# Two PSUM tiles for the attention's banks, gate columns stored as rows, tied splits, and four pairs of modulations in one bank each

## The chip, the cores and the metric

The kernel runs on one core of a Trainium2 chip. The metric is the device time of one execution in microseconds (us). An engine works through its own instruction queue in order: TensorE (PE; its weight loads are PEld), VectorE (DVE), ScalarE (ACT), GpSimd (POOL) and SyncE (SP), the last of which only issues transfers. Work on different engines is ordered by semaphores alone: an instruction waits until a counter of another engine has reached a value, and that value names the instruction that must have ended.

## The reference

The kernel computes one layer of a block for a diffusion model, on 512 latent tokens and 256 context tokens with 2048 channels, all in float32:

```
shift, scale, gate = split(silu(c) @ w_ada + b_ada, 3)         # c: 2048, w_ada: 2048 x 6144
h  = rmsnorm(x)   * (1 + scale)   + shift                      # 512 x 2048
hc = rmsnorm(ctx) * (1 + scale_c) + shift_c                    # 256 x 2048, from c_ctx
p = h @ w_in                                                   # q, k, v, z_a, u_b, z_b, g_a, g_b
q, k = rope(rmsnorm(q)), rope(rmsnorm(k)); kc, vc from hc @ w_in
attn = softmax(q @ [k, kc].T) @ [v, vc]                        # 12 heads of 128, 4 key heads, 768 keys
y_a = (attn * silu(z_a)) @ w_pa
y_b = (real(fft2(u_b)) * silu(z_b)) @ w_pb
y = (sigmoid(g_a) * y_a + sigmoid(g_b) * y_b) @ w_o
out = rmsnorm(x + gate * y) * final_g
```

## The kernel before

A float32 product is made of three products of rounded halves: an operand is split by `split_from` (L181, L182) into a high part on ScalarE and a low part on VectorE, and `mm3` (L339 to L341) adds high times high, high times low and low times high in a PSUM bank. The large products are done by a scheme of seven block products (`Group`, named P1 to Q6), whose sums and differences VectorE and ScalarE take from PSUM (L1109, L1116, L1121, L1649).

The program has four stages. Up to some 128 us the rows are normed and modulated. `modulate(kb)` multiplies c and c_ctx with 256 columns of w_ada (`matvec`, L567), copies the result out (L583), turns it with two transposes (L588) and reduces it (L599) to the shift and the gain of the 128 channels of row kb. `row_hi` (L618) and `row_lo` (L625) then write the two halves of that row of h, and the first products (L680 to L687) begin with row 0. Then the large input products run to some 803 us, in PSUM tiles of a pool `psp`. The attention follows, to some 1003 us; then two branch groups and two output groups, to the end.

At the attention's start that pool is closed, and one tile of all eight banks is taken (L1462 to L1466). Six banks are `banks[0]`. Four score regions of 768 columns (`wide`) lie in them, the fourth for transposes. Of the two in `banks[1]`, one is an accumulator for the filler (products of the other branch that are put between the steps) and the other takes the value sums.

A step of the attention is one head and 128 queries, 48 steps in all. `scores(i)` makes six products into one of three regions, VectorE takes the maximum (L1533), ScalarE the exponential with its sum (L1535). `turn(i - 1)` makes six transposes into the fourth region (L1551), which are split into `pth` (ScalarE, L181) and `ptl` (VectorE, L182). `values` (every second step) makes 18 products of 256 columns with them in the other tile, and turns two blocks of the gate (L1566), which ScalarE copies (L1576) and VectorE multiplies in (L1577). Beside them run the turning of queries and keys (L1396, L1389), gates (`use_gate`, L1369) and splits of later weights.

No table orders the work. A scheduler of the language places the instructions of each engine and puts in the waits, from what each instruction reads and writes; `issue_after` ties one instruction behind another. Behind the attention the same tiles serve the branch and output groups, through `pair`: each product takes two neighbouring banks in turn.

Of the kernel before, what the change touches and what calls it, by code (L numbers as in the profile page):

```python
# [18 lines left out]
P = 128  # L19
D = 2048  # L20
T = 512
C = 256
KK = D // P
# [4 lines left out]
NKEY = T + C  # L28
KT = NKEY // P
# [94 lines left out]
def block_kernel(ctx, tc, xT, ctx_rows, ctx_toks, x, c_row, w_ss, w_gate, vecs, qkg, rope, dft_c, dft_s,  # L124
                 w_start, w_g, w_pab, w_o, final_g, out):
    nc = tc.nc
# [6 lines left out]
    const = sb("const")  # L133
# [9 lines left out]
    gs = dsc.tile([KK, P], F32, name="gs")  # L143
# [13 lines left out]
    def uid(s):  # L157
        cnt[0] += 1
        return f"{s}{cnt[0]}"
# [14 lines left out]
    def bank2():  # L174
        return ps.tile([P, 512], F32, tag="b2", bufs=2, name=uid("pd"))
# [4 lines left out]
    def split_from(src, hi, lo):  # L180
        first = nc.scalar.activation(hi, src, ACT.Copy)  # L181
        return first, nc.vector.tensor_tensor(lo, src, hi.bitcast(F32), op=ALU.subtract)  # L182
# [76 lines left out]
    last_split, split_of, in_line, context_sub, chained = [], [], [], [], []  # L259

    look = [1]

    def split_piece(e):
        if e.out is not None or e.kind == "raw":
            return
        raws = [r for _, r in e.raws]
        src = raws.pop(0) if e.stage is None else chain[e.pc]
        for r in raws:
            nc.vector.tensor_tensor(src, src, r, op=ALU.add)
        if e.off:  # L270
            with ExitStack() as line:
                if e.key == ("P7", KV, 3):
                    line.enter_context(tc.issue_after(context_sub[-1].ins))
                if e.key[1] in DIFF_IN_LINE:

                    line.enter_context(tc.issue_after(split_of[-2][1].ins))
                nc.vector.tensor_tensor(src, chain[e.pc], src, op=ALU.subtract)
        hi, lo = e.dst() if e.dst else hl_tiles()
        if isinstance(hi, Halves):
            for k in range(2):  # L280
                last_split.append(split_from(src[:, 512 * k : 512 * k + 512].rearrange("p (a c) -> p a c", a=2),
                                             hi.parts[k], lo.parts[k]))
        else:
            hi, lo = hi[:, : e.cols], lo[:, : e.cols]
            with ExitStack() as line:
                if in_line:
                    for i in last_split[-1]:
                        line.enter_context(tc.issue_after(i.ins))
                last_split.append(split_from(src, hi, lo))
        split_of.append(last_split[-1])  # L290
        if e.nxt is not None:
            chained[:] = [nc.gpsimd.dma_start(chain[e.pc], e.nxt, accum_op=ALU.add)]  # L292
# [67 lines left out]
    gcol = const.tile([P, KK], F32, name="gcol")  # L360
    gparts = const.tile([P, 2 * KK], F32, name="gparts")

    pairs = []
# [81 lines left out]
    q = NGATE  # L445
# [39 lines left out]
    def load_start():  # L485

        may[0] = 1
        with tc.issue_after(last_load[0]):
            load_more()
        assert not may[0]  # L490
        last_load[0] = asked[0].ins

    def wada_load(kb):
        r = []
        for h in range(2):
            r.append(pap.tile([P, 8, 256], F32, tag="wada", bufs=4, name=uid("wa")))
# [24 lines left out]
    fch = ppool.tile([P, 2, 2 * P], F32R, name="fch")  # L521
# [38 lines left out]
            nc.tensor.matmul(acc[:, t * P : t * P + P], pick[:, t, :], r, start=True, stop=True)  # L560
        return acc

    def matvec(kb, h):
        acc, w = two[kb][:, :256], wada[kb][h]
        for k in range(8):
            j, n = k % 4, 8 * h + k
            nc.tensor.matmul(acc[32 * j : 32 * j + 32], c2[:, n, :], w[:, k, :], start=n < 4, stop=n >= KK - 4)  # L567

    o_of, sp_of = {}, {}

# [2 lines left out]
    def modulate(kb, meanwhile=lambda: None):  # L573
        two[kb] = bank2()
        for h in range(2):
            matvec(kb, h)
        meanwhile()
        return taken(kb)

    def taken(kb):  # L580
        o = o_of[kb] = pap.tile([P, 256], F32, tag="ada_o", bufs=2, name=uid("ado"))
        wada.pop(kb)
        return nc.scalar.copy(o, two[kb][:, :256])  # L583

    def turned(kb):
        o = o_of.pop(kb)
        for i in range(2):
            nc.tensor.transpose(two[kb][:, 256 + P * i : 256 + P * i + P], o[:, P * i : P * i + P], ident)  # L588
        if kb == 0:
            warm(3, o)  # L590

    def columns(kb):
        turned(kb)
        factors(kb)

    def factors(kb):
        sp = two.pop(kb)[:, 256:]
        r = pap.tile([P, 2, 2], F32, tag="ada_r", bufs=2, name=uid("adr"))
        nc.vector.tensor_reduce(r, sp.rearrange("p (h g r) -> p h r g", h=2, g=4)[:, :, 0:2, :], axis=AX.X, op=ALU.add)  # L599
        nc.vector.tensor_scalar(gain[:, kb, :], r[:, 1, :], bsc1[:, kb : kb + 1], ng[:, kb : kb + 1],  # L600
                                op0=ALU.add, op1=ALU.mult)
        last = nc.vector.tensor_scalar(shift[:, kb, :], r[:, 0, :], bada[:, kb : kb + 1], None, op0=ALU.add)
        return last

    rx0, y_of = [], {}

    def rows_of(kb):
        if kb % 2 == 0:
# [6 lines left out]

    def row_hi(kb):
        rows_of(kb)
        nc.scalar.activation(hhi[kb], y_of[kb], ACT.Identity, bias=shift[:, kb, 0:1], scale=gain[:, kb, 0:1])  # L618

    def scaled(kb):  # L620
        nc.vector.tensor_scalar(xt[:, kb, :], y_of.pop(kb), gain[:, kb, 0:1], None, op0=ALU.mult)

    def row_lo(kb):
        v = xt[:, kb, :]
        nc.vector.scalar_tensor_tensor(hlo[kb], v, shift[:, kb, 0:1], hhi[kb].bitcast(F32),  # L625
                                       op0=ALU.add, op1=ALU.subtract)

    def make_h(kb, meanwhile=lambda: None):
        rows_of(kb)
# [147 lines left out]
    with tc.manual_schedule(engines={E.PE}):  # L777
# [6 lines left out]
        with tc.manual_schedule(engines={E.Activation, E.DVE}):  # L784
# [59 lines left out]
            for kb in range(4, KK - 4, 2):  # L844
                some(3)
                split_next()
                some(5)
                split_next()
                if kb == 6:
                    rotations()  # L850
                k = kb + 2
                for i in range(2):
                    modulate(k + i)
                    if k + 2 + i < KK:
                        wada[k + 2 + i] = wada_load(k + 2 + i)
                        for _ in range(2 if k + 2 + i == KK - 3 else 1):
                            load_start()
                some(1)
                for i in range(2):
                    turned(k + i)  # L860
# [686 lines left out]
    def turn(i):  # L1547
        p = probs.pop(i)
        tp = wide[3]
        for k in range(KT):  # L1550
            nc.tensor.transpose(tp[:, k * P : (k + 1) * P], p[:, k * P : (k + 1) * P], ident)  # L1551
# [518 lines left out]
```

## Time and profile before

| | |
|---|---|
| median of 3 runs | 1285.94 us (1285.69 to 1288.67) |
| the profiled execution | 1286.97 us, span 1285.2 us |
| granted TensorE clock | 0.999 |
| busy: PE, DVE, ACT, POOL | 1269.6, 991.0, 683.2, 173.2 us |
| first and last transpose of the attention | 809.7 and 1003.2 us |
| transfers | 319.07 MB, mean 248 GB/s |

A line of the waits names the engine, the line and tile that waited, the instruction that ended the wait, the sum, the count and the longest. A line of the groups gives busy time and mean duration in ns, and behind the bar the idle time of the engine just ahead with what ended it. In the table by windows, the engines follow the length in the order PE, PEld, DVE, ACT, POOL, and then the granted clock, the share of the transfer engines and GB/s.

### The profile page before, as it was taken

What the parts mean: (1) busy time and instruction counts of PE and PEld (TensorE: products, weight loads), DVE (VectorE), ACT (ScalarE), POOL (GpSimd) and SP (SyncE); (2) the same over time, 40 slices, a digit from 0 to 9 for tenths busy, and PEclk for the clock granted to TensorE, in tenths of its full rate; (3) what the DMA queues carried; (4) which work ended last, traced back from release to release, by engine and by line L of the source; (5) the groups of instructions that cost most, each with busy time, mean ns of one, the idle gap of its engine ahead of it and who ended that gap; (6) DMA issues with size and microseconds to landing.
All of it is one profiled execution on the core that took longest, in us unless ns stands there. A gap on an engine that the chain in (4) does not pass through costs nothing.

```text
span 1285.2 us, 17638 instructions
## 1 busy us (share of the span) xinstructions
PE 1269.6 (99%) x6562; PEld 1045.2 (81%) x6562; DVE 991.0 (77%) x1305; ACT 683.2 (53%) x1077; POOL 173.2 (13%) x226
## 2 busy tenths in 40 slices
PE   8999999999999999999999999999999999999997
PEld 5677888888888888888888888888888888888886
DVE  5767899889778787748687756778898777787677
ACT  5322765555466564543355445766667646465544
POOL 0000121111102011012021011011100221211310
PEclk9999999999999999999999999999999999999999
DMA  9998798888898998887879897578852989998986
GB/s 378 412 368 344 242 204 254 229 240 239 234 315 209 320 271 254 291 197 188 282 204 288 254 259 234 180 234 250 265 178 67 260 241 258 245 207 222 227 207 179
DMA packets 104343, 319.07 MB, mean 248 GB/s; under 512 B 9889, under 2 KB 32801, under 8 KB 100289
## 3 DMA queue, kind: packets, MB, share of 16 engines
q1 hardware_dynamic: 54336, 195.24, 41.8%
q0 software_dynamic: 27600, 100.29, 37.0%
q10 hardware_dynamic: 22320, 22.42, 5.1%
q8 instruction: 51, 0.84, 0.3%
q14 instruction: 36, 0.29, 0.1%
HBM read 283.30 MB, written 34.61 MB: 247 GB/s over the span
## 4 chain that ended last, share of the span: by engine, by line
PE 82%; DVE 3%; DMA 2%; ACT 2%; issue 1%; SPq 0%; ACTq 0%
PE banks L339 10%; PE banks L340 10%; PE banks L341 10%; PE x L341 9%; PE x L339 9%; PE x L340 9%; PE y L341 8%; PE y L340 8%; PE y L339 8%; PE banks L1551 2%; DMA wr<-in_w_pab 1%; DVE wlo L182 1%; DMA s<-yb_d 1%; PE banks L1665 1%; DVE s L182 0%
## 5 line engine op out<-in xcount | busy, mean ns | idle before, releaser
L181 ACT ACTIVATE whi<-R 128x1024 fp32r<-128x1024 f32 x138 | 145.1, 1058 | 143.7 <-PE banks L341 47.5
L182 DVE TENSOR_TENSOR wlo<-R,whi 128x1024 fp32r<-128x1024 f32 x138 | 167.7, 1221 | 61.2 <-ACT whi L181 60.9
L182 DVE TENSOR_TENSOR wlo<-wr,whi 128x1024 fp32r<-128x1024 f32 (+1 forms) x122 | 147.3, 1213 | 62.7 <-ACT whi L181 62.5
L181 ACT ACTIVATE whi<-wr 128x1024 fp32r<-128x1024 f32 (+1 forms) x122 | 127.4, 1050 | 123.4 <-PE y L341 33.0
L339 PE MATMUL banks<-whi,s 128*128 128x512 f32 (+1 forms) x400 | 157.8, 394 | 0.9 <-ACT ev L1160 0.7
L340 PE MATMUL banks<-wlo,s 128*128 128x512 f32 (+1 forms) x400 | 155.9, 390 | 0.0
L341 PE MATMUL banks<-whi,s 128*128 128x512 f32 (+1 forms) x400 | 155.8, 389 | 0.0
L339 PE MATMUL x<-whi,s 128*128 128x512 f32 x352 | 137.1, 390 | 0.0
L341 PE MATMUL x<-whi,s 128*128 128x512 f32 x352 | 137.0, 389 | 0.0
L340 PE MATMUL x<-wlo,s 128*128 128x512 f32 x352 | 136.9, 389 | 0.0
L292 POOL DMA_DIRECT2D R<-in_w_g x68 | 59.5, 874 | 484.7 <-DVE wlo L182 290.2
L340 PE MATMUL y<-wlo,s 128*128 128x512 f32 x316 | 123.0, 389 | 0.1
L339 PE MATMUL y<-whi,s 128*128 128x512 f32 x316 | 122.9, 389 | 0.0
L341 PE MATMUL y<-whi,s 128*128 128x512 f32 x316 | 122.8, 389 | 0.0
L181 ACT ACTIVATE s<-wr 128x512 fp32r<-128x512 f32 (+2 forms) x93 | 60.8, 677 | 66.0 <-DMA wr<-cf_d 24.4
L182 DVE TENSOR_TENSOR s<-wr,s 128x512 fp32r<-128x512 f32 (+2 forms) x93 | 66.7, 749 | 31.8 <-ACT s L181 30.9
L339 PEld LDWEIGHTS banks<-whi,s 128*128 128x128 f32 x400 | 75.2, 188 | 16.6 <-ACT ev L1160 1.1
L341 PEld LDWEIGHTS banks<-whi,s 128*128 128x128 f32 x400 | 75.2, 188 | 15.3
L340 PEld LDWEIGHTS banks<-wlo,s 128*128 128x128 f32 x400 | 75.2, 188 | 13.9 <-DVE wlo L182 0.2
L340 PEld LDWEIGHTS x<-wlo,s 128*128 128x128 f32 x352 | 66.1, 188 | 13.8
L341 PEld LDWEIGHTS x<-whi,s 128*128 128x128 f32 x352 | 66.1, 188 | 13.7
L339 PEld LDWEIGHTS x<-whi,s 128*128 128x128 f32 x352 | 66.1, 188 | 13.6
(333 smaller groups left out, 2794.0 us busy)
## 6 DMA issues: line engine op xcount, KB each, us to landing
wr<-in_w_g SPq DMA_DIRECT2D x124, 512.0 KB, 5.6
R<-in_w_g POOLq DMA_DIRECT2D x68, 512.0 KB, 7.4
wa<-in_w_ss SPq DMA_DIRECT2D x31, 1024.0 KB, 9.5
R<-in_w_g SPq DMA_DIRECT2D x32, 512.0 KB, 5.8
wr<-in_w_gate SPq DMA_DIRECT2D x32, 512.0 KB, 5.1
wr<-in_w_o SPq DMA_DIRECT2D x24, 512.0 KB, 7.1
R<-in_w_o POOLq DMA_DIRECT2D x24, 512.0 KB, 8.9
wr<-in_w_pab SPq DMA_DIRECT2D x20, 512.0 KB, 6.1
```

Source lines behind the costliest of these rows:

```text
L181: first = nc.scalar.activation(hi, src, ACT.Copy)
L182: return first, nc.vector.tensor_tensor(lo, src, hi.bitcast(F32), op=ALU.subtract)
L292: chained[:] = [nc.gpsimd.dma_start(chain[e.pc], e.nxt, accum_op=ALU.add)]
L339: nc.tensor.matmul(o, ah, bh, start=start, stop=False, skip_group_check=cont)
L340: nc.tensor.matmul(o, ah, bl, start=False, stop=False, skip_group_check=cont)
L341: nc.tensor.matmul(o, al, bh, start=False, stop=stop, skip_group_check=cont)
L1551: nc.tensor.transpose(tp[:, k * P : (k + 1) * P], p[:, k * P : (k + 1) * P], ident)
L1665: last_turn[0] = nc.tensor.transpose(tp[:, k // 2, 256 * (k % 2) + P * t : 256 * (k % 2) + P * t + P], m[:, t, k * P : k * P + P], ident)
```

## The change

Five edits. (1) The one tile of eight banks becomes two tiles, of six and of two banks. The banks have the same shapes and the same uses. (2) The 16 gate columns are turned by VectorE (in blocks of 32 by 32) and stored by four transfers of 16 rows of 32, in place of one transfer of single elements. (3) A split of the branch weights `pab` is tied behind an earlier split of the transposes (`turned_low`). (4) Rows 6 to 13 are modulated in four pairs: the second row's product is added into the same bank, through a copy of c shifted by two columns (zeros elsewhere), so that one copy, two transposes and one reduction serve two rows. (5) Row 0 is written in four blocks of 128 tokens by `row_hi` and `row_lo`.

```diff
@@ split_piece
-                if in_line:
-                    for i in last_split[-1]:
-                        line.enter_context(tc.issue_after(i.ins))
+                for i in last_split[-1] if in_line else turned_low[-6:-4] if e.key[0] == "pab" else ():
+                    line.enter_context(tc.issue_after(i.ins))
@@ 
-    c2 = pap.tile([P, KK, 32], F32, name="c2")
+    c2 = pap.tile([P, KK, 34], F32, name="c2")
-    nc.vector.tensor_tensor(c2[:, :, 0:2].rearrange("p k j -> p j k"),
+    nc.vector.tensor_tensor(c2[:, :, 2:4].rearrange("p k j -> p j k"),
...
-    def matvec(kb, h):
-        acc, w = two[kb][:, :256], wada[kb][h]
+    def matvec(kb, h, first=True, last=True):
+        acc, w, c = two[kb][:, :256], wada[kb][h], c2[:, :, 2:34] if first else c2[:, :, 0:32]
...
+    def modulate_pair(kb, loads):
+        two[kb] = two[kb + 1] = bank2()
+        for i in range(2):
+            for h in range(2):
+                matvec(kb + i, h, i == 0, i == 1)
+            if i:
+                taken(kb)
+            wada.pop(kb + i, None)
+            loads(kb + i)
...
+    tokens_of = lambda kb: [slice(P * t, P * t + P) for t in range(4)] if kb == 0 else [slice(0, T)]
...
     def row_hi(kb):
         rows_of(kb)
-        nc.scalar.activation(hhi[kb], y_of[kb], ACT.Identity, bias=shift[:, kb, 0:1], scale=gain[:, kb, 0:1])
+        for c in tokens_of(kb):
+            nc.scalar.activation(hhi[kb][:, c], y_of[kb][:, c], ACT.Identity, bias=shift[:, kb, 0:1], scale=gain[:, kb, 0:1])
...
-    whole_psum = psq.tile([P, 8, 512], F32, name="banks")
-    banks += [whole_psum[:, :6, :], whole_psum[:, 6:, :]]
+    banks += [psq.tile([P, n, 512], F32, name=f"banks{n}") for n in (6, 2)]
...
-        split_from(tp[:, :NKEY].rearrange("p (k q) -> p k q", k=KT), *(w[:, :, c] for w in pts[i // 2]))
+        turned_low.extend(split_from(tp[:, :NKEY].rearrange("p (k q) -> p k q", k=KT), *(w[:, :, c] for w in pts[i // 2])))
...
-    nc.vector.tensor_tensor(gcol, gparts[:, :KK], gparts[:, KK:], op=ALU.add)
-    nc.vector.tensor_tensor(gcol, gcol, bada[:, 2 * KK :], op=ALU.add)
-    nc.gpsimd.dma_start(gs.rearrange("k p -> p k"), gcol)
+    nc.vector.tensor_tensor(gparts[:, :KK], gparts[:, :KK], gparts[:, KK:], op=ALU.add)
+    nc.vector.tensor_tensor(gparts[:, :KK], gparts[:, :KK], bada[:, 2 * KK :], op=ALU.add)
+    nc.vector.transpose(gcol, gparts)
+    for i in range(0, P, 32):
+        nc.gpsimd.dma_start(gs[:, i : i + 32], gcol[i : i + KK, :])
```

Lines of the changed kernel stand up to 22 higher: L1551 becomes L1571, L1533 and L1535 become L1553 and L1555, L1109 becomes L1130, L1121 becomes L1142, L1649 becomes L1669, and L339 to L341 become L338 to L340.

The edit of the tiles also changes the waits. On TensorE, in the attention, these rows stood in the program before (`L339` to `L341` with `s886` and `s887` are score products, with `whi884` the filler's, `L1551` and `L1566` transposes of probabilities and gate; a row's waits stand in brackets, by the engine's counter):

```order
L1566 MATMUL banks_6439<-ident_86,s870_6648 128x128 x2
L339 MATMUL banks_6439<-s886_6820,s908_6998 128x256
L340 MATMUL banks_6439<-s887_6821,s908_6998 128x256
L341 MATMUL banks_6439<-s886_6820,s908_6998 128x256
L339 MATMUL banks_6439<-s886_6820,s908_6998 128x512
L340 MATMUL banks_6439<-s887_6821,s908_6998 128x512
L341 MATMUL banks_6439<-s886_6820,s908_6998 128x512
L339 MATMUL banks_6439<-whi884_6810,s839_6393 128x512 [waits DVE_49]
L1551 MATMUL banks_6439<-ident_86,s913_7064 128x128 [waits DVE_49]
L1551 MATMUL banks_6439<-ident_86,s913_7064 128x128 x5
L340 MATMUL banks_6439<-wlo885_6811,s839_6393 128x512
L341 MATMUL banks_6439<-whi884_6810,s840_6394 128x512
```

and these stand there now, in the same part of the attention (score products have `s874` and `s875`, the filler `whi872`):

```order
L1571 MATMUL banks6_6417<-ident_86,s900_6994 128x128 [waits Activation_49]
L1571 MATMUL banks6_6417<-ident_86,s900_6994 128x128 x5
L1586 MATMUL banks2_6418<-ident_86,s858_6627 128x128
L338 MATMUL banks6_6417<-s874_6799,s896_6977 128x512 [waits DVE_49]
L339 MATMUL banks6_6417<-s875_6800,s896_6977 128x512
L340 MATMUL banks6_6417<-s874_6799,s896_6977 128x512
L338 MATMUL banks6_6417<-s874_6799,s896_6977 128x256
L339 MATMUL banks6_6417<-s875_6800,s896_6977 128x256
L340 MATMUL banks6_6417<-s874_6799,s896_6977 128x256
L338 MATMUL banks2_6418<-whi872_6789,s827_6371 128x512 [waits DVE_49]
L339 MATMUL banks2_6418<-wlo873_6790,s827_6371 128x512
L340 MATMUL banks2_6418<-whi872_6789,s828_6372 128x512
```

Before, the score products carry no wait of their own here; now the first of them waits for a counter of VectorE, and the filler's first product (`whi872`) too.

On ScalarE, the order in the same place was (`L1535` is the exponential, `L181` with `pth` the split of the transposes):

```order
L1535 ACTIVATE s912_7015,gain_102<-banks_6439,gain_102 128x768 [waits DVE_49]
L1576 COPY R3_1342<-banks_6439 128x256 [waits PE_49]
L1545 ACTIVATE s870_6648<-s870_6648,gain_102 128x128 [waits DVE_49]
L181 ACTIVATE pth906_6988<-banks_6439 128x6x128 [waits PE_49]
L1545 ACTIVATE s870_6648<-s870_6648,gain_102 128x128 [waits DVE_49]
L1535 ACTIVATE s916_7089,gain_102<-banks_6439,gain_102 128x768 [waits DVE_49,Activation_49]
L1535 ACTIVATE s913_7064,gain_102<-banks_6439,gain_102 128x768 [waits DVE_49]
L181 ACTIVATE pth914_7075<-banks_6439 128x6x128 [waits PE_49,Activation_49]
```

and now is:

```order
L1555 ACTIVATE s900_6994,gain_102<-banks6_6417,gain_102 128x768 [waits DVE_49]
L1565 ACTIVATE s858_6627<-s858_6627,gain_102 128x128 [waits DVE_49]
L181 ACTIVATE pth894_6967<-banks6_6417 128x6x128 [waits PE_49]
L1555 ACTIVATE s901_7043,gain_102<-banks6_6417,gain_102 128x768 [waits DVE_49,Activation_49]
L1565 ACTIVATE s858_6627<-s858_6627,gain_102 128x128 [waits DVE_49]
L181 ACTIVATE pth902_7054<-banks6_6417 128x6x128 [waits PE_49,Activation_49]
L1596 COPY R3_1320<-banks2_6418 128x256 [waits PE_49]
```

Two exponentials stood one behind the other before; now exponential and split of the transposes alternate.

Behind the attention, at the start of a product of an output group, TensorE's rows were:

```order
L340 MATMUL banks_6439<-wlo1261_9777,s1230_9621 128x512
L341 MATMUL banks_6439<-whi1260_9776,s1231_9622 128x512
L339 MATMUL banks_6439<-whi1263_9795,s1171_9247 128x512 [waits Activation_49]
L340 MATMUL banks_6439<-wlo1264_9796,s1171_9247 128x512 [waits DVE_49]
L341 MATMUL banks_6439<-whi1263_9795,s1172_9248 128x512
```

and are now:

```order
L339 MATMUL banks6_6417<-wlo1249_9760,s1218_9604 128x512
L340 MATMUL banks6_6417<-whi1248_9759,s1219_9605 128x512
L338 MATMUL banks6_6417<-whi1251_9778,s1159_9230 128x512 [waits DVE_49,Activation_49]
L339 MATMUL banks6_6417<-wlo1252_9779,s1159_9230 128x512
L340 MATMUL banks6_6417<-whi1251_9778,s1160_9231 128x512
```

A new product (`whi1263` before, `whi1251` now) waited only for a counter of ScalarE; now it waits for VectorE as well.

More of the change, by code (lines that the diff above doesn't have):

```diff
@@ L256, in hl_tiles @@
         return [pool.tile([P, 1024], F32R, tag=t, bufs=hl_pools.count(pool), name=uid("w" + t)) for t in ("hi", "lo")]
-    last_split, split_of, in_line, context_sub, chained = [], [], [], [], []
+    last_split, split_of, in_line, context_sub, chained, turned_low = [], [], [], [], [], []
     look = [1]
@@ L359, in block_kernel @@
     gain = const.tile([P, KK, 2], F32, name="gain")
-    gcol = const.tile([P, KK], F32, name="gcol")
+    gcol = const.tile([P, 2 * KK], F32, name="gcol")
     gparts = const.tile([P, 2 * KK], F32, name="gparts")
@@ L561, in spread @@
         return acc
-    def matvec(kb, h):
-        acc, w = two[kb][:, :256], wada[kb][h]
+    def matvec(kb, h, first=True, last=True):
+        acc, w, c = two[kb][:, :256], wada[kb][h], c2[:, :, 2:34] if first else c2[:, :, 0:32]
         for k in range(8):
             j, n = k % 4, 8 * h + k
-            nc.tensor.matmul(acc[32 * j : 32 * j + 32], c2[:, n, :], w[:, k, :], start=n < 4, stop=n >= KK - 4)
+            nc.tensor.matmul(acc[32 * j : 32 * j + 32], c[:, n, :], w[:, k, :], start=first and n < 4,
+                             stop=last and n >= KK - 4, skip_group_check=not (first and last))
     o_of, sp_of = {}, {}
@@ L578, in modulate @@
         return taken(kb)
+    def modulate_pair(kb, loads):
[7 more added lines that the diff above has]
+            loads(kb + i)
     def taken(kb):
         o = o_of[kb] = pap.tile([P, 256], F32, tag="ada_o", bufs=2, name=uid("ado"))
-        wada.pop(kb)
+        wada.pop(kb, None)
         return nc.scalar.copy(o, two[kb][:, :256])
@@ L594, in columns @@
         factors(kb)
+    r_of = {}
     def factors(kb):
         sp = two.pop(kb)[:, 256:]
-        r = pap.tile([P, 2, 2], F32, tag="ada_r", bufs=2, name=uid("adr"))
-        nc.vector.tensor_reduce(r, sp.rearrange("p (h g r) -> p h r g", h=2, g=4)[:, :, 0:2, :], axis=AX.X, op=ALU.add)
+        if kb not in r_of:
+            n = 4 if kb + 1 in two else 2
+            r = pap.tile([P, 2, 4], F32, tag="ada_r", bufs=2, name=uid("adr"))
+            nc.vector.tensor_reduce(r[:, :, :n], sp.rearrange("p (h g r) -> p h r g", h=2, g=4)[:, :, 0:n, :],
+                                    axis=AX.X, op=ALU.add)
+            r_of[kb] = r[:, :, 0:2]
+            if n == 4:
+                r_of[kb + 1] = r[:, :, 2:4]
+        r = r_of.pop(kb)
         nc.vector.tensor_scalar(gain[:, kb, :], r[:, 1, :], bsc1[:, kb : kb + 1], ng[:, kb : kb + 1],
@@ L623, in row_lo @@
     def row_lo(kb):
-        v = xt[:, kb, :]
-        nc.vector.scalar_tensor_tensor(hlo[kb], v, shift[:, kb, 0:1], hhi[kb].bitcast(F32),
-                                       op0=ALU.add, op1=ALU.subtract)
+        for c in tokens_of(kb):
+            nc.vector.scalar_tensor_tensor(hlo[kb][:, c], xt[:, kb, c], shift[:, kb, 0:1], hhi[kb][:, c].bitcast(F32),
+                                           op0=ALU.add, op1=ALU.subtract)
     def make_h(kb, meanwhile=lambda: None):
@@ L851, in block_kernel, with loads @@
                 k = kb + 2
[L852 to L857, printed above, removed]
+                def loads(k):
+                    wada[k + 2] = wada_load(k + 2)
+                    for _ in range(2 if k + 2 == KK - 3 else 1):
+                        load_start()
+                modulate_pair(k, loads)
                 some(1)
-                for i in range(2):
-                    turned(k + i)
+                turned(k)
                 factors(k)
```

## The prediction

> **What bounds the kernel now.** I read the page's busy times first, then the table by windows, then the list of TensorE's waits. The first line and the slices of the page:
>
> ```profile
> span 1285.2 us, 17638 instructions
> PE 1269.6 (99%) x6562; PEld 1045.2 (81%) x6562; DVE 991.0 (77%) x1305; ACT 683.2 (53%) x1077; POOL 173.2 (13%) x226
> PE   8999999999999999999999999999999999999997
> ```
>
> TensorE is busy for 1269.6 of 1285.2 us, so 15.6 us of idle time is all that any better overlap can win. Every wait that reaches TensorE is paid in full. The windows say where that idle time lies (PE busy is the first number behind the colon):
>
> ```profile
> 16.00:24.00 8.00, 6.67 (x69) 4.53 (x61) 4.51 (x9) 3.29 (x6) 0.00 (x0) 1.00 1.03 413
> 800.00:832.00 32.00, 31.32 (x189) 26.75 (x189) 24.16 (x37) 21.89 (x39) 3.02 (x5) 1.00 0.56 176
> 832.00:864.00 32.00, 30.74 (x212) 26.93 (x211) 25.78 (x42) 20.79 (x42) 4.64 (x8) 1.00 0.79 253
> 864.00:896.00 32.00, 31.93 (x217) 27.78 (x216) 26.61 (x42) 21.10 (x41) 5.53 (x9) 1.00 0.79 237
> 960.00:992.00 32.00, 32.00 (x214) 28.24 (x213) 27.59 (x49) 22.30 (x45) 1.80 (x3) 1.00 0.27 83
> 1024.00:1280.00 256.00, 253.00 (x1164) 209.10 (x1162) 197.91 (x190) 135.88 (x164) 47.15 (x57) 1.00 0.90 224
> ```
>
> The attention stage (800 to 1003 us) runs TensorE almost without a gap, although a softmax passes over three engines in every step. The waits confirm it:
>
> ```profile
> PE banks L1389 <- DVE ptl L182: 0.8, 1, 0.8
> PE banks L339 <- ACT ev L1160: 0.7, 1, 0.7
> PE banks L1551 <- DVE ptl L182: 0.4, 1, 0.4
> PE banks L339 <- ACT s L1535: 0.4, 1, 0.4
> ```
>
> The attention has 48 steps (12 heads by 4 blocks of 128 queries). Its transposes give the pace:
>
> ```profile
> L1551 PE MATMUL banks<-ident,s x288: 270/273/332, 809.7 to 1003.2; 128*128 128x128 f32 x144
> ```
>
> First to last start is 193.5 us over 47 steps, or 4.12 us a step. One step in the timeline, taken from 880 to 890 us, shows why no gap opens:
>
> ```profile
> 880.17 0.28 PE L339 MATMUL banks<-s,s 128*128 128x256 f32 x1
> 880.40 0.28 PE L341 MATMUL banks<-s,s 128*128 128x256 f32 x1
> 880.73 0.96 DVE L1533 TENSOR_REDUCE gain<-banks 128x1 f32<-128x768 f32 x1
> 881.23 0.39 PE L339 MATMUL banks<-s,s 128*128 128x512 f32 x1
> 881.46 0.39 PE L340 MATMUL banks<-s,s 128*128 128x512 f32 x1
> 881.60 0.95 DVE L182 TENSOR_TENSOR ptl<-banks,pth 128x768 fp32r<-128x768 f32 x1
> 884.97 0.90 ACT L1535 ACTIVATE s<-banks,gain 128x768 f32<-128x768 f32 x1 [0.58 <-DVE gain L1533]
> 885.77 0.19 ACT L1535 ACTIVATION_READ_ACCUMULATOR s<-banks,gain 128x1 f32 x1
> 886.68 0.82 PE L1551 MATMUL banks<-ident,s 128*128 128x128 f32 x6
> 887.53 0.82 ACT L181 ACTIVATE pth<-banks 128x768 fp32r<-128x768 f32 x1 [0.28 <-PE banks L1551]
> ```
>
> TensorE writes a later step's scores (881.23) while VectorE still takes an earlier step's maximum (880.73) and reads its transposes (881.60): three steps are in work at once, each in banks of its own. The chain of one step is longer than 4.12 us and is hidden by that.
>
> **The two tiles.** The order of the changed program shows this edit to be no mere renaming. With one tile of eight banks, a score product waits only for the last readers of its own bank. With a tile of six banks, the first score product of each step waits for VectorE, the first transpose for ScalarE, and ScalarE's rows alternate exponential and split. The value that each wait carries names the instruction: the scores wait for the low split `ptl` of the transposes just ahead of them, and the transposes for the exponential of the scores just ahead, though they lie in other banks. All accesses of the six banks are thus ordered as if they were one region. The same holds in the two-bank tile between the filler's accumulator and the value sums. What was three steps deep becomes one chain:
>
> - scores: three products of 512 columns at 0.23 us pitch (881.23 to 881.46) and three of 256 from 880.17 to the last one's end at 880.68 (0.51): 1.20. A first product behind a gap costs about 0.1 more (the transposes' longest is 332 against a median of 273 ns, and its weights load uncovered before it): 1.3.
> - maximum, 0.96.
> - exponential to the end of its accumulator read, 885.96 less 884.97: 0.99.
> - six transposes, 0.82 (with a gap ahead 0.87).
> - high split, 0.82.
> - low split, 0.95.
> - six handovers between engines, 0.03 to 0.05 each (the split starts at 887.53, after transposes that end at 887.50): 0.25.
>
> The sum is 6.1 us a step. The value sums, the filler's products and the gate's transposes now fit into the two gaps of each step (maximum and exponential, 2.0; the two splits, 1.8), since TensorE's own work is 4.12 us a step, of which the chain holds 2.2. Over 47 steps, the chain takes 288 us. Three heads' groups need their keys turned (L1389), and those transposes with their splits form a further link. A transposition's 0.82, its two splits of 0.8 and 0.95 and handovers are 2.8 each, so 8. Every step also has other work in the queues of ScalarE and VectorE that is in the way now and then:
>
> ```profile
> L181 ACT ACTIVATE whi<-wr 128x1024 fp32r<-128x1024 f32 x6 | 6.4, 1059 | 2.9 <-DMA wr<-in_w_pab 2.9
> L1369 DVE SCALAR_TENSOR_TENSOR wr<-wr,crow 128x1024 f32<-128x1024 f32 x16 | 19.4, 1214 | 0.0
> L182 DVE TENSOR_TENSOR wlo<-wr,whi 128x1024 fp32r<-128x1024 f32 x7 | 8.5, 1218 | 0.8 <-ACT whi L181 0.8
> ```
>
> Some 30 such instructions of 1.1 to 1.2 us run in these 200 us. If one in six delays the chain by its whole length, that is 6. If none does, 0; if all do, 35. So the stage takes 288 + 8 + 6 = 302 in place of 193.5: **+109 us**, with bounds 288 - 193.5 = +95 and +138.
>
> **Product starts behind the attention.** The branch and output groups write a product into one pair of banks while the previous pair is being read. In the order, some seventeen first products now wait for the reading of the pair just finished (most of them for VectorE beside ScalarE), where only a weight split was waited for. Its price stands in the timeline of the stage, with the tail's first and last readings of the banks:
>
> ```profile
> 1025.64 1.02 ACT L1121 COPY s<-banks 128x1024 f32<-128x1024 f32 x1 [1.66 <-PE banks L341]
> 1042.86 1.23 DVE L1109 TENSOR_TENSOR s<-banks,s 128x1024 f32<-128x1024 f32 x1 [0.40 <-PE banks L341]
> ```
>
> A bare wait is the reading, 1.02 or 1.23, with two handovers and the restart (0.2) and the last product's tail (0.39 less a pitch of 0.23): 1.4 to 1.6. Where other products of the order stand between, less remains, about 0.5. In two places the named subtraction is the last of four VectorE instructions of 1.23 in a row, 4.9. I take fifteen at 1.4 and two at 4.9: **+31 us**. Low bound: fifteen at 0.5 and two at 1.6, 11; high bound: fifteen at 1.6 and two at 6.2, 36.
>
> **The tail.** The last sums share the tile, so VectorE's first reading can no longer start ahead of the last product:
>
> ```profile
> 1272.00 0.69 DVE L1930 TENSOR_TENSOR s<-banks,s 128x512 f32<-128x512 f32 x1
> 1277.71 0.42 DVE L1930 TENSOR_TENSOR s<-banks,s 128x256 f32<-128x256 f32 x1
> ```
>
> The first would move to where the last stands, 5.7 at most; nothing if the squares on ScalarE set the end anyway. I take nearer to the whole shift, as the readings follow each other on VectorE: **+5**, bounds 0 and 6.
>
> **Start and small edits.** Four pairs lose eight transposes, four copies and four reductions:
>
> ```profile
> L583 ACT COPY ado<-pd 128x256 f32<-128x256 f32 x16 | 6.0, 372 | 30.6 <-PE pd L567 30.5
> L588 PE MATMUL pd<-ident,ado 128*128 128x128 f32 x32 | 5.5, 274 | 0.5 <-ACT ado L583 0.5
> L599 DVE TENSOR_REDUCE adr<-pd 128x4 f32<-128x16 f32 x16 | 2.7, 169 | 5.0 <-PE pd L588 5.0
> ```
>
> Only the transposes are on TensorE: pitch 0.11 each (0.44 for two less the last one's tail), so -0.9 us. The wider matrix of c costs a memset that nothing waits for; the copies and reductions are hidden behind TensorE's products and give nothing. Row zero in four blocks turns one activation of 0.82 into four:
>
> ```profile
> L618 ACT ACTIVATE s<-S,shift,gain 128x512 fp32r<-128x512 f32 x6 | 4.9, 816 | 8.9 <-DVE shift L602 8.9
> L1349 ACT ACTIVATE qr<-qr,shift 128x128 f32<-128x128 f32 x8 | 2.8, 393 | 1.1 <-DVE qr L1340 1.1
> PE pb L680 <- ACT s L618: 0.3, 1, 0.3
> ```
>
> A block of 128 takes about 0.39, so four take 1.2 to 1.6, and the first product can start 0.3 to 0.4 earlier, which wins the 0.3 of its wait. But the split of the weights queued behind (768 columns, 22.32 to 23.15, its low part 23.18 to 24.14) is what TensorE's product at 24.20 needs, so that is 0.4 to 0.8 later: about +0.3, bounds -0.3 and +0.8. The tied splits hold a branch weight's split back behind the two splits of an earlier step's transposes, which the chain now makes late anyway; what they can win are the waits quoted above, 2.3 us together, and I take -1, bounds -2.3 and 0. The gate column's four transfers replace one on POOL's queue, with one VectorE transpose. POOL is busy 13% and the row is read only for the output groups, so this costs 0; uncovered, three more issues at some 0.9 us each, the duration of POOL's commonest issue on the page, would cost 2.7:
>
> ```profile
> L292 POOL DMA_DIRECT2D R<-in_w_g x68 | 59.5, 874 | 484.7 <-DVE wlo L182 290.2
> ```
>
> **Sum.** 109 + 31 + 5 - 0.9 + 0.3 - 1 = +143. The profiled execution took 1286.97 us (span 1285.2), 1.0 above the median of 1285.94; on the median this gives **1429 us**.
>
> **The rivals.**
>
> *The waits cost nothing and the small edits show.* The whole tile would then be a tidier name: -0.9 for the pairs, -1 for the splits, 1284 us; with all 2.3 us of the quoted waits, 1282.7. Here speaks the trace, in which TensorE never waits more than 0.8 us in this stage. Against it: the waits of before are other waits, and the new ones name instructions that cannot have run by then. It holds if the score products' new wait ends before TensorE gets there. The Trainium skill, "PSUM — Partial Sum Buffer", section "PSUM bank collisions raise a hardware error", asks for a guard by bank and quadrant only. By that rule the waits between the scores' and the transposes' banks are needless, and the sum would be this rival's 1284. But the chip obeys the program's waits, not the rule; no run here shows them yet. Chance 0.05: 0.03 faster, 0.02 no difference that can be measured.
>
> *Attention serial, products hidden.* If the seventeen starts find their banks read by then, because ScalarE and VectorE are free (POOL and ACT have slack there), and the low bounds of the other terms hold: 95 + 11 + 0 - 1 = +105, 1391 us. For it: ACT is 53% busy. Against: TensorE is the engine that finishes last, so it comes to a start at once. Chance 0.10.
>
> *TensorE's clock falls.* Each step leaves two gaps of up to 2 us. All windows quoted have a granted clock of 1.00, also 16 to 24 us, where PE idled 1.33 of 8 us. If it halved in the attention, TensorE's own 4.12 a step would be 8.2, 47 steps would take 387 and the stage +193 in place of +109: 1513 us. Chance 0.04. The Trainium skill, "TensorE: Matmul & The Clock Gate", section "A second HAM failure mode: psum-queue depth-cycling", tells of just this (short idle times between groups that swing the clock between half and full), while its section "HAM oscillation — how this bites in real kernels" asks for idle gaps above some 3.4 us, and by that the clock would stay. The trace of before agrees with the second so far as its short gaps go.
>
> *Queues in the way in most steps.* All 30 long instructions delay the chain: +138 + 36 + 6 = +180, 1466 us. Chance 0.06.
>
> **How the numbers follow.** The forecast, all terms within the bounds, has 0.75. For the range I take 1396 to 1462: most of the forecast's own spread and part of the second and fourth rival. Slower by over 0.3%, which is about what a measurement of this kernel can tell from no change, has 0.75 + 0.10 + 0.04 + 0.06 = 0.95.
>
> **What would show it.** TensorE's busy time stays near 1269 while its share falls below 90%. The transposes' first and last starts lie about 300 us apart, ended by ScalarE's exponential; the score products' idle time is ended by the low split, each over 1 us a step. ScalarE's exponentials come one by one. Behind the attention, first products wait for L1130, L1142 and L1669. If the transposes' distance stays at 194 us, the main step is wrong; if it is 300 and the stage behind is as long as before, only the second term is.

## The result, and the profile after

The changed kernel takes 1476.59 us in the median of 6 runs (1472.88 to 1481.18), the kernel before 1286.06 us. The ratio is 1.148 with a 95% interval of 1.1455 to 1.1505: slower by 190 us, where 143 were forecast, and 14.6 us above the range.

The head of the page after, with the granted clock of TensorE in tenths over the 40 slices:

```profile
span 1479.4 us, 17623 instructions
PE 1338.2 (90%) x6554; PEld 1082.2 (73%) x6554; DVE 999.8 (68%) x1305; ACT 689.8 (47%) x1076; POOL 175.5 (12%) x229
PE   8999999999999999999999667777777888898996
PEclk9999999999999999999999899787988999999998
```

Up to some 800 us the slices are as before. Then TensorE has gaps, as forecast. But its busy time has also grown, by 69 us with eight products fewer, and its clock is no longer full. TensorE's longest waits after, over the whole span:

```profile
PE banks L338 <- DVE ptl L182: 49.6, 45, 2.9
PE banks L1571 <- ACT s L1555: 19.6, 16, 2.1
PE banks L338 <- DVE s L1130: 15.2, 6, 4.8
PE banks L338 <- ACT pth L181: 10.3, 12, 1.2
PE banks L1685 <- DMA s<-yb_d: 6.5, 5, 3.9
PE banks L1410 <- DVE ptl L182: 5.4, 3, 1.8
```

The first row is the wait for the low split of the transposes ahead, 45 times, 43 of them by scores; the second is the transposes' wait for the exponential. Both were read from the order. The transposes again give the attention's length:

```profile
L1571 PE MATMUL banks<-ident,s x288: 270/273/477, 813.5 to 1148.0; 128*128 128x128 f32 x144
```

Their first and last start are now 334.5 us apart. The two traces, cut at the same instructions:

| stretch | before | after | forecast | measured |
|---|---|---|---|---|
| start to the first product in the attention's banks | 803.6 | 803.8 | -1.6 | +0.2 |
| from there to the first transpose | 6.1 | 9.7 | 0 | +3.6 |
| first to last transpose | 193.5 | 334.5 | +109 | +141.0 |
| last transpose to TensorE's last product | 274.5 | 318.9 | +31 | +44.4 |
| from there to the end of the span | 7.5 | 12.5 | +5 | +5.0 |
| span | 1285.2 | 1479.4 | +143 | +194.2 |

What the forecast lacked lies mostly in two stretches, 32 us in the attention and 13 behind it. Over 45 of the steps, the chain measured in the trace is this (each link from its start to its end; all time between the links is in the row of handovers):

| link, mean us | forecast | after |
|---|---|---|
| six score products | 1.3 | 1.63 |
| maximum | 0.96 | 0.96 |
| exponential with its read | 0.99 | 0.99 |
| six transposes | 0.87 | 0.94 |
| high split, low split | 1.77 | 1.77 |
| handovers and other work in the way | 0.25 | 0.87 |
| step, mean (median, least) | 6.1 | 7.16 (6.88, 6.10) |

The least step is 6.10 us, against the forecast's 6.1. The row of handovers also holds the turning of keys and the other work in the queues, which the forecast priced apart at 8 and 6 us, 0.30 a step: its 0.87 stands against 0.55. Of that, 0.25 is the transposes' wait behind the exponential, where a bare handover is 0.05. The maximum, exponential and splits are what the rows of before said. The score products are not: in 17 of the 45 steps they take 1.8 to 2.29 us in place of 1.31. One such step (2.13 us), first in the timeline of TensorE (880 to 890 us), with its late transposes (0.60 us behind the exponential) and the next step's scores behind it:

```profile
880.80 0.42 PE L338 MATMUL banks<-s,s 128*128 128x256 f32 x1 [0.61 <-DVE ptl L182]
...
881.45 0.63 PE L338 MATMUL banks<-s,s 128*128 128x512 f32 x1
881.88 0.63 PE L339 MATMUL banks<-s,s 128*128 128x512 f32 x1
882.30 0.63 PE L340 MATMUL banks<-s,s 128*128 128x512 f32 x1
882.73 0.41 PE L339 MATMUL banks<-ptl,s 128*128 128x256 f32 x1
...
885.62 0.82 PE L1571 MATMUL banks<-ident,s 128*128 128x128 f32 x6
...
888.39 0.50 PE L338 MATMUL banks<-s,s 128*128 128x512 f32 x1 [1.84 <-DVE ptl L182]
888.72 0.40 PE L339 MATMUL banks<-s,s 128*128 128x512 f32 x1
888.96 0.39 PE L340 MATMUL banks<-s,s 128*128 128x512 f32 x1
```

and then in the table by windows of the same time (the granted clock is the third number from the end):

```profile
879.00:880.00 1.00, 0.19 (x1) 0.19 (x1) 0.21 (x1) 0.76 (x1) 0.00 (x0) 1.00 0.68 131
880.00:881.00 1.00, 0.39 (x2) 0.20 (x2) 0.75 (x1) 0.00 (x0) 0.02 (x1) 1.00 0.03 4
881.00:882.00 1.00, 1.00 (x5) 0.90 (x5) 0.00 (x0) 0.00 (x0) 0.53 (x1) 0.51 0.00 0
882.00:883.00 1.00, 1.00 (x5) 0.81 (x4) 0.03 (x1) 0.00 (x0) 0.00 (x0) 0.50 0.92 377
883.00:884.00 1.00, 1.00 (x6) 1.00 (x6) 1.00 (x2) 0.00 (x0) 0.00 (x0) 0.50 0.37 148
884.00:885.00 1.00, 1.00 (x8) 1.00 (x8) 1.00 (x2) 0.98 (x2) 0.00 (x0) 0.78 0.00 0
```

A product of 512 columns has a pitch of 0.43 us at the clock of 0.50 (881.45 to 881.88), and of 0.24 at full clock (888.72 to 888.96). Over the attention, the clock records of this trace show 20 such stretches of half clock, nearly all of 3.4 or 6.8 us and 96 us together; before there are none in this stage. All 17 steps with slow scores lie in these stretches, and no step outside them has slow scores.

### The profile page after: what moved, and what is told of

It reads as the page before. It is cut to its first block, busy times and chain, and to the rows that moved or that the text cites. A ratio compares the mean times of both kernels' runs of the same rounds, so it can differ in the third digit from the quotient of the medians.

```text
span 1479.4 us, 17623 instructions
## 1 busy us (share of the span) xinstructions
PE 1338.2 (90%) x6554; PEld 1082.2 (73%) x6554; DVE 999.8 (68%) x1305; ACT 689.8 (47%) x1076; POOL 175.5 (12%) x229
## 4 chain that ended last, share of the span: by engine, by line
PE 79%; DVE 7%; DMA 5%; ACT 5%; issue 3%; POOL 1%; SPq 0%; ACTq 0%; POOLq 0%; DVEq 0%
PE banks L338 9%; PE banks L339 8%; PE banks L340 8%; PE x L340 7%; PE x L339 7%; PE x L338 7%; PE y L339 6%; PE y L340 6%; PE y L338 6%; DVE ptl L182 3%; PE banks L1571 3%; ACT pth L181 2%; DMA s<-yb_d 2%; PE pd L566 2%; PE pc L338 1%
## 5 line engine op out<-in xcount | busy, mean ns | idle before, releaser
L181 ACT ACTIVATE whi<-R 128x1024 fp32r<-128x1024 f32 x138 | 145.4, 1058 | 155.8 <-PE banks L340 79.0
L181 ACT ACTIVATE whi<-wr 128x1024 fp32r<-128x1024 f32 (+1 forms) x122 | 127.2, 1050 | 148.3 <-PE banks L340 53.3
L338 PE MATMUL banks<-whi,s 128*128 128x512 f32 (+1 forms) x400 | 166.6, 416 | 32.3 <-DVE s L1130 15.2
L339 PE MATMUL banks<-wlo,s 128*128 128x512 f32 (+1 forms) x400 | 162.0, 405 | 0.0
L340 PE MATMUL banks<-whi,s 128*128 128x512 f32 (+1 forms) x400 | 161.5, 404 | 0.0
L338 PE MATMUL x<-whi,s 128*128 128x512 f32 x352 | 137.3, 390 | 0.0
L339 PE MATMUL x<-wlo,s 128*128 128x512 f32 x352 | 137.1, 390 | 0.0
L340 PE MATMUL x<-whi,s 128*128 128x512 f32 x352 | 137.1, 390 | 0.0
L339 PE MATMUL y<-wlo,s 128*128 128x512 f32 x316 | 123.3, 390 | 0.6 <-DVE wlo L182 0.6
L338 PE MATMUL y<-whi,s 128*128 128x512 f32 x316 | 123.1, 390 | 0.0
L340 PE MATMUL y<-whi,s 128*128 128x512 f32 x316 | 122.9, 390 | 0.0
L338 PEld LDWEIGHTS banks<-whi,s 128*128 128x128 f32 x400 | 79.3, 198 | 56.4 <-ACT whi L181 14.6
L338 PE MATMUL banks<-s,s 128*128 128x512 f32 (+1 forms) x160 | 66.7, 417 | 46.7 <-DVE ptl L182 46.7
L1555 ACT ACTIVATE s<-banks,gain 128x768 f32<-128x768 f32 x48 | 43.2, 901 | 130.9 <-DVE gain L1553 127.3
L181 ACT ACTIVATE s<-wr 128x512 fp32r<-128x512 f32 (+2 forms) x93 | 60.4, 676 | 69.7 <-DMA wr<-cf_d 23.9
L182 DVE TENSOR_TENSOR ptl<-banks,pth 128x768 fp32r<-128x768 f32 x48 | 45.9, 957 | 69.1 <-ACT pth L181 69.1
L340 PEld LDWEIGHTS banks<-whi,s 128*128 128x128 f32 x400 | 78.9, 197 | 17.4
L339 PEld LDWEIGHTS banks<-wlo,s 128*128 128x128 f32 x400 | 79.5, 199 | 14.6
```

The source lines that it names most:

```text
L338: nc.tensor.matmul(o, ah, bh, start=start, stop=False, skip_group_check=cont)
L339: nc.tensor.matmul(o, ah, bl, start=False, stop=False, skip_group_check=cont)
L340: nc.tensor.matmul(o, al, bh, start=False, stop=stop, skip_group_check=cont)
L1555: maxima[1] = nc.scalar.activation(probs[i], sc[:, :NKEY], ACT.Exp, bias=mx[:, 0:1], accum_out=mx[:, 1:2])
```

## The experiments

Two theories stood against each other for the missing part: that the clock falls because TensorE idles in every step, and that waits and queues cost more than the forecast had them. Ahead of that stood the question whether the two tiles are the whole loss.

**The tiles alone.** The kernel before, with only this edit:

```diff
-    whole_psum = psq.tile([P, 8, 512], F32, name="banks")
-    banks += [whole_psum[:, :6, :], whole_psum[:, 6:, :]]
+    banks += [psq.tile([P, n, 512], F32, name=f"banks{n}") for n in (6, 2)]
```

> The kernel before with the two tiles alone; nothing else of the change. If the waits of the two tiles are the whole loss: 1470 to 1482 us, attention (first to last transpose) 330 to 340 us. If the small edits carry a part of it (the gate column's four transfers, the tied splits, the paired rows): more than 8 us below the changed kernel's 1476.6.

Measured: 1482.81 us (1476.77 to 1483.66), ratio 1.1509 (1.1489 to 1.1529). First to last transpose 336.8 us. The median is 0.8 us above the expected range, the attention is within its own, and the ratio's interval overlaps with the changed kernel's (1.1455 to 1.1505): the two tiles are the whole loss.

**All but the tiles.** The changed kernel, with that edit undone:

> The changed kernel with the one tile of eight banks put back: all small edits, without the two tiles. If the tiles are the whole loss: within 3 us of the kernel before, 1283 to 1288 us, since in the changed kernel the first product in the attention's banks began at 803.76 us and in the one before at 803.6. If the small edits cost something that the tiles hide: above 1290 us.

Measured: 1285.5 us (1284.9 to 1288.57), ratio 0.9990 (0.9981 to 0.9998). The small edits together cost nothing; they win about a thousandth.

**The clock.** To hold the clock up, TensorE must do more work in the gaps, in banks that nothing else uses. The changed kernel has none, so the control divides the eight banks into tiles of four, two and two. Scores have one region and transposes one in the first tile; the second is empty during the attention:

```diff
+    four = psq.tile([P, 4, 512], F32, name="banksa")
+    spare = psq.tile([P, 2, 512], F32, name="banksb")
+    duo = psq.tile([P, 2, 512], F32, name="banksc")
...
+    banks += [four[:, :2, :], four[:, 2:, :], spare, duo]
+    wide = [flat(banks[i])[:, :NKEY] for i in (0, 0, 0, 1)]
```

> The kernel before with three tiles of 4, 2 and 2 banks: one region for scores and one for transposes share the four, the tile of two in the middle stays empty during the attention, so the attention is the same single chain and only the product starts behind it wait less often. Both theories: attention 325 to 345 us. In total 1460 to 1475 us. It is the control for the next run.

Measured: 1464.05 us (1463.26 to 1471.48), ratio 1.1392 (1.1367 to 1.1418). First to last transpose 330.7 us, the mean step 7.08 us with scores of 1.63: the same chain with the same half clock. A second version of this control adds work that nothing reads:

```diff
+    def keep_busy(behind):
+        with tc.issue_after(behind.ins):
+            for k in range(8):
+                nc.tensor.transpose(spare[:, 0, (k % 4) * P : (k % 4) * P + P], ident, ident)
...
+        if i % 2 or i < 4:
+            keep_busy(last_score)
...
+        keep_busy(last_turned)
```

> The same three tiles, with 8 more transposes of 128 columns (0.87 us at full clock) into the empty tile behind the transposes of every step, and 8 behind the scores of every second step: extra work on TensorE that nothing reads. Theory that the clock falls because TensorE idles in each step: the granted clock rises to 0.97 or more in the attention, scores and transposes are back to 1.3 and 0.87 us in every step, and the attention gets shorter by 15 to 35 us although TensorE does 60 us more. Theory that the loss above the forecast is only waits and queues: no shorter, up to 15 us longer.

Measured: 1439.37 us (1438.47 to 1439.98), ratio 1.1181 (1.1166 to 1.1196): 24.7 us faster than its control, with 592 more products on TensorE. Two windows of the control:

```profile
864.00:896.00 32.00, 22.97 (x109) 19.30 (x107) 12.32 (x20) 11.01 (x21) 3.54 (x6) 0.76 0.46 138
992.00:1024.00 32.00, 23.36 (x128) 19.26 (x129) 15.17 (x23) 11.93 (x22) 3.04 (x5) 0.89 0.44 132
```

and the same two with the added work, and its transposes:

```profile
864.00:896.00 32.00, 27.02 (x176) 23.34 (x175) 15.71 (x25) 12.61 (x23) 4.42 (x7) 0.95 0.57 161
992.00:1024.00 32.00, 28.65 (x200) 24.70 (x199) 18.34 (x28) 15.02 (x28) 1.07 (x2) 1.00 0.33 114
```

```profile
L1560 PE MATMUL banksa<-ident,s x288: 270/273/459, 812.4 to 1120.7; 128*128 128x128 f32 x144
```

The clock is back at 1.00 in most windows (two stretches at half, 6.8 us together, against 19 and 82 us), and the transposes are 308.3 us apart, 22.4 less. The mean step falls from 7.08 to 6.58 us: scores 1.63 to 1.34, transposes 0.91 to 0.88, the transposes' wait behind the exponential 0.23 to 0.08 (the value sums that fill this gap fit again), the rest 0.03. So the clock is shown as a cause, and holding it up wins 22 us of this control's attention. Some 14 of them are the scores and transposes themselves, which run at twice the pace where the clock is full again. The rest, most of it the transposes' wait, is put down to the clock with less certainty, because the scheduler also ordered some of ScalarE's and VectorE's work differently in this run. The three turns of keys now wait 2.8 us each, 8.5 together where 8 were forecast. What is left above the forecast is 308.3 - 302 = 6.

**Tiles by role.** Four tiles of two banks: a score region each in two of them (two regions in place of three), the transposes in the third, filler and value sums in the fourth. A pair of the product groups is one tile:

```diff
+    trio = [psq.tile([P, 2, 512], F32, name=f"banks{n}") for n in "abc"]
+    duo = psq.tile([P, 2, 512], F32, name="banksd")
...
+    banks += trio + [duo]
+    wide = [flat(banks[i])[:, :NKEY] for i in (0, 1, 0, 2)]
...
-            return banks[0][:, b : b + 2, :] if b < 6 else banks[1]
+            return banks[b // 2]
```

> The kernel before with four tiles of two banks each: one for each of two score regions (of before's three), one for the transposes, one for the filler's accumulator and the value sums together. Each tile is again waited for as a whole, but scores, transposes and the pairs of the product groups no longer share one. Theory that it is the sharing of a tile by neighbours in the chain that costs, not the number of tiles: attention 195 to 215 us, granted clock 0.99 or more, no waits for the reading of a pair behind the attention (that stage 275 to 282 us), 1287 to 1310 us in all. Rival, that several tiles cost in themselves or that a missing third score region costs a step's depth: above 1330 us.

Measured: 1298.97 us (1298.11 to 1299.57), ratio 1.0093 (1.0079 to 1.0107). Its transposes, its waits behind the attention, and the attention's windows:

```profile
L1552 PE MATMUL banksc<-ident,s x288: 270/272/329, 810.3 to 1006.7; 128*128 128x128 f32 x144
```

```profile
PE banksa L339 <- ACT s L1114: 2.4, 2, 1.7
PE banksc L339 <- ACT s L1121: 1.2, 1, 1.2
PE banksd L1666 <- DMA s<-yb_d: 1.1, 1, 1.1
```

```profile
832.00:1024.00 192.00, 187.51 (x1229) 165.81 (x1228) 158.53 (x258) 127.74 (x242) 28.18 (x45) 1.00 0.66 203
```

The attention is 196.4 us, 2.9 more than before, at a clock of 1.00. Four tiles cost about 1% where two tiles cost 15%: what costs is that neighbours of one chain share a tile. The filler's accumulator and the value sums still share one here, as in the changed kernel, so the prediction's point that they too are ordered by their tile is worth at most these 2.9 us while the clock is full. From the last transpose to TensorE's last product it takes 280.8 us (274.5 before); of the waits for the reading of a pair 3.6 us remain, and the long ones for L1109 (L1130 in the changed kernel) are gone. In the control of three tiles that stage took 305.8, in the changed kernel 318.9: the more pairs share a tile, the longer. Why the scheduler tells the banks of one tile of eight apart and not those of a tile of six was not tried.

**The small edits, one by one.** Each is taken back in the changed kernel with one tile of eight banks (1285.5 us with all of them).

```diff
-    tokens_of = lambda kb: [slice(P * t, P * t + P) for t in range(4)] if kb == 0 else [slice(0, T)]
+    tokens_of = lambda kb: [slice(0, T)]
```

> The changed kernel with one tile of eight banks, and row 0 written in one piece again. By the forecast's term for the row in four blocks (+0.3, bounds -0.3 and +0.8): 0.3 us below the run with all small edits (1285.5), at most 0.8 below. If the blocks win time: above it.

Measured: 1285.05 us (1284.06 to 1285.88), ratio to the kernel before 0.9986 (0.9978 to 0.9995).

```diff
-                for i in last_split[-1] if in_line else turned_low[-6:-4] if e.key[0] == "pab" else ():
+                for i in last_split[-1] if in_line else ():
```

> The changed kernel with one tile of eight banks, and the splits of the branch weights not tied. By the forecast's term for the ties (-1, bounds -2.3 and 0): 1 us above the run with all small edits, at most 2.3 above.

Measured: 1286.49 us (1285.92 to 1287.38), ratio 0.9996 (0.9988 to 1.0005).

```diff
-                modulate_pair(k, loads)
+                for i in range(2):
+                    modulate(k + i)
+                    loads(k + i)
...
-                turned(k)
+                for i in range(2):
+                    turned(k + i)
```

> The changed kernel with one tile of eight banks, and the eight rows modulated one by one again. By the forecast's term for the pairs (-0.9): 0.9 us above the run with all small edits. Rival: the first stage waits for its weights' transfers (their share is about 1 there), so that saved products win nothing and the times are equal.

Measured: 1286.35 us (1285.68 to 1288.67), ratio 0.9997 (0.9988 to 1.0006).

The differences from 1285.5, 0.45 below, 1.0 above and 0.85 above, have the sign and about the size of the three terms (0.3, 1, 0.9); by the ratios, each against the kernel before of its own session, they are 0.5, 0.8 and 0.9. But the intervals are wider than the ratios are apart, so no single edit's share is shown, and the agreement may be luck. The version with one tile and without the four blocks is the fastest measured, clear of the kernel before by its interval.

## Why the prediction was right or wrong

**The bound, right.** TensorE had no slack, and every wait that reached it was paid. The sign that its busy time would stay near 1269 us did not hold: it rose to 1338.2. The product starts' own price is an example of a wait that was paid: four VectorE instructions in a row were to make 4.9 us, and the timeline after shows them one by one:

```profile
1196.62 1.23 DVE L1130 TENSOR_TENSOR s<-banks,s 128x1024 f32<-128x1024 f32 x1 [0.40 <-PE banks L340]
1197.76 1.22 DVE L182 TENSOR_TENSOR wlo<-wr,whi 128x1024 fp32r<-128x1024 f32 x1
1198.89 1.22 DVE L1130 TENSOR_TENSOR s<-s,s 128x1024 f32<-128x1024 f32 x1
1200.03 1.22 DVE L1130 TENSOR_TENSOR s<-s,banks 128x1024 f32<-128x1024 f32 x1
1201.38 0.47 PE L338 MATMUL banks<-whi,s 128*128 128x512 f32 x1 [4.81 <-DVE s L1130]
```

**The mechanism, right.** Scores wait for the low split, transposes for the exponential, one chain a step. The tiles alone give the whole loss, and a step that nothing disturbs takes 6.10 us against the 6.1 of the sum. One reading was too simple: the regions are not each in banks of their own. A region of 768 columns is one and a half banks, so the third score region shares a bank with the transposes, and the first two share one. In the kernel before, no transpose waits over 0.4 us all the same.

**The attention's term, too small: +109 against +141.** The step that failed is the one behind the chain, "TensorE's own work is 4.12 us a step" and so fits into the gaps. It holds at full clock only. The rival had it that the clock falls, but gave this 0.04, and priced it as one state for the whole stage (1513 us). In truth the clock is at half for 96 of 334 us, in stretches of 3.4 us or a multiple, each begun after TensorE had been busy for 0.37 to 0.56 of the 3.4 us ahead. By the table, the 32 us missing are some 15 in the scores, 3 in the transposes, 9 in the transposes' wait behind the exponential and 5 in the three turns of keys, which wait 3.3, 4.4 and 5.5 us, 13 in place of 8. The first two are half clock by the records. Of the third, all but 0.4 us lies in steps with a stretch at half clock, where the value sums ahead of the transposes run at half pace. Of the turns, only the two longer ones lie in such a stretch; why the control, at full clock, once waits 3.7 us there is open. The forecast's guess of 6 us for other work in the queues held in this trace. In the run with added work it was some 4 too small.

Of the Trainium skill, "TensorE: Matmul & The Clock Gate", section "A second HAM failure mode: psum-queue depth-cycling", was the right one, and I set it aside for the section on idle gaps above 3.4 us. The longest idle time of TensorE in the attention is 2.9 us (the scores' row of the waits), and the clock fell all the same. The evidence that I took from before was one window with TensorE busy for 6.67 of 8 us, which is not sparse enough to speak for a chain that by the forecast keeps TensorE busy for 4.1 of 6.4 us, and in single stretches of 3.4 us for less than half. The mean share hides this. Cut into stretches of 3.41 us in step with the clock's changes, the attention of the changed kernel has 17 at full clock with TensorE busy for less than 0.50, and half clock followed all of them. It followed 3 of 8 between 0.50 and 0.56, and none of the 45 above. (In the control, three stretches of 0.46 to 0.47 stayed at full clock, so the edge is not sharp.)

**The product starts, +31 against +44.** The waits for the reading of a pair and for the splits ahead of a product (the rows of the list in that stage) sum to 25 us, less than the 31. Two costs were not in the sum. The transposes of the merged halves (L1685) wait 6.5 us for their accumulating transfer, where before it was 0.7, and 1.1 with tiles by role; why that transfer comes later against TensorE was not tried. And TensorE's busy time in the stage grew from 274 to 287 us, with a granted clock of 0.94 to 0.97 in its first 160 us:

```profile
1184.00:1216.00 32.00, 26.67 (x114) 21.58 (x113) 17.93 (x15) 9.64 (x11) 4.21 (x6) 0.95 0.73 174
1248.00:1280.00 32.00, 26.32 (x118) 21.31 (x119) 21.79 (x19) 15.38 (x15) 5.44 (x7) 0.95 0.94 240
```

Four stretches at half clock, 17 us together, make up to 8.5 of the 13 us of busy time, and first products behind a gap the rest. This is argued from the records; no run held the clock up there.

**Small terms.** The tail is +5.0, as forecast, and by the step that was named: VectorE's first reading, 5.7 us ahead of the end of TensorE's last product before, now stands right behind it (1466.89):

```profile
1466.92 0.69 DVE L1952 TENSOR_TENSOR s<-banks,s 128x512 f32<-128x512 f32 x1 [2.12 <-PE banks L340]
```

The first steps' chain, 3.6 us more until the first transpose, was put at nothing. The start's -1.6 did not come in this trace (+0.2), while the run with all small edits and one tile is about 1 us below the kernel before by its ratio. The gate column's four transfers cost nothing that can be seen.

**The range** ended at 1462, because a clock that falls in part was no case of its own: it was priced as full or as half for the whole stage.

## What to carry to other kernels

Before dividing a tile, look at what the scheduler then waits for: a tile may be the unit of the waits, and neighbours of a pipelined chain should not share one unless its banks are told apart. When a change opens gaps on TensorE in a stage, look at its busy share in single stretches of some 3.4 us and not at the mean; where stretches fall to about a half, price their work at a falling clock as well as at a full one, in stretches, not as one state. A chain's price from single rows held (6.1 us); what surrounds it has to be bounded more widely.

## What the hardware showed that was not expected

Work that nobody reads made the kernel faster: 592 products on TensorE for 24.7 us less (1464.05 to 1439.37). In the changed kernel's attention, the clock fell to one half after stretches in which TensorE was busy for 0.37 to 0.56 of 3.4 us, although no gap was longer than 2.9 us, and it stayed there for 3.4 us or a multiple of it. In the kernel before, with TensorE busy nearly throughout, it did not fall in this stage.
